# First transposes between products of ones, and the parts of x~ pinned in order

## Chip, cores and metric

The kernel runs on one core of a Trainium2 chip, as one launch. The metric is device microseconds of that core. PE is the matrix engine (PEld its weight loads), DVE, ACT and POOL are the vector, scalar and general engines, SP issues most of the DMAs.

## The reference

Two layers of a bidirectional encoder over x of 256 tokens by 1024 channels, all float32. Each layer has three stages, each with its own RMSNorm:

```
x += 0.5 * SwiGLU(RMSNorm(x))            # stage 3l:   1024 -> 2 x 2816 -> 1024
z  = RMSNorm(x) @ W_in                   # stage 3l+1: the mixer
x += concat(attention, pooling, HGRN2 of z) @ W_out
x += 0.5 * SwiGLU(RMSNorm(x))            # stage 3l+2
...
rmsnorm(x, g) = x * rsqrt(mean(x * x) + EPS) * g
swiglu(h)     = (silu(h @ w_gate) * (h @ w_up)) @ w_down
```

The change touches how x, times the gain g, gets to the matrix engine at the start of every stage, and the beginning of the program above all.

## The kernel before

**Products in three parts.** A float32 product is made as three products of a rounded format: each operand is split into a high part (ACT writes it, rounded) and a low part (DVE subtracts the high part from the original). Weights come from HBM in halves of 128 x 1024 (`feed_dma`, L133, SP queue, four `stage` buffers) and are split into `whi` (ACT, L149) and `wlo` (DVE, L150), up to `LOOK` = 4 halves ahead (`ahead`, `split_part`). The first half of all is fetched and split in two pieces. `mm3t` (L168 to L170) then makes high x high, high x low and low x high.

**x~, the turned activations.** At each stage x has to lie with its channels on the partitions. `turn(stage, dh, tt)` transposes four 128 x 128 tiles of one token half `tt` on PE (L294) into PSUM tiles `xps`; each `xps` tile is one bank and holds two channel tiles k of 256 tokens each: `xps[0]` has k = 0 and 1, `xps[1]` has 2 and 3. With the second token half, `turn` calls `parts` for its four k: ACT writes the high part `xh` = rounded x * g (L272), DVE the low part `xl` (L273); both read the bank. The normalising factor is left out of x~ and applied to the products later: `squares` (ACT, L281) sums x * x, `rms` makes `rc` of it, and the gate's Silu scales with `rc`. The fourth `squares` of a stage is followed by a preload of another activation table.

**PSUM.** A pool of four banks (`g`) serves `idle`, the `xps`, the accumulators `gu` (two a block, one for each token half), `hp` and others; a bank is given again when the readers of its last tile are done. At a later stage's start four `xps` tiles hold all four, and the next stage's first accumulators (`gu`, in the mixer `ga` and `gb`) take the first banks that come free.

**Order.** The instructions of PE and SP stand in the order in which they are written. Those of ACT and DVE are ordered by a planner when the program is built, from data dependences and its own costs; `issue_after(ins)` ties the instructions in its block that are on the engine of `ins` behind `ins`, without a semaphore.

**SwiGLU.** `ffn` runs over 11 blocks of 256 columns. `gate_up` makes one block's `gu` in four quarters of 12 products (two k, two token halves, three parts). Quarter q uses k = 2q and 2q + 1 and weight half i0 + q. In quarter 1 the held back `turn` of the second channel half runs (`late_turn`); in the first stage `sums`, which calls the four `squares`, is called in quarter 3. In the mixer, `proj_pair` starts with `ga` and `gb` side by side.

**The beginning** (`body`): twelve 128 x 128 products of ones into `idle` (two PE records each), the split of the first weight half, the two turns of the first channel half, DMAs up to half 5, then the first stage, with the second channel half in `second`.

Of the kernel before, what the change touches and what calls it, by code (L numbers as in the profile page):

```python
# [8 lines left out]
F32 = mybir.dt.float32  # L9
F32R = mybir.dt.float32r  # L10
U8 = mybir.dt.uint8
AF = mybir.ActivationFunctionType
ALU = mybir.AluOpType
# [3 lines left out]
P = 128  # L17
# [24 lines left out]
HALF = 1024  # L42
# [28 lines left out]
class Trunk:  # L71
    def __init__(self, ctx, tc, x_in, wall, prm_in, rel_in, cst_in, cst2_in, msk_in, band_in, y_out):
        self.tc, self.nc = tc, tc.nc
        self.wall, self.y_out = wall, y_out
        nc = self.nc
        pool = lambda name, bufs=1, **k: ctx.enter_context(tc.tile_pool(name=name, bufs=bufs, **k))
        self.cp = pool("const")
        self.stg = pool("stage", 4)
        self.whl = pool("whl", LOOK + 1)
        self.xp = pool("xp")  # L80
        self.wk = pool("wk", 2)
        self.mx = pool("mx")
        self.pg = pool("pg", 4, space=PSUM)
        self.py = pool("py", 4, space=PSUM)
        self.dr = pool("dr", space=DRAM)

        self.stage_t, self.split_t = {}, {}
        self.n_dma = 0
        self.n_split = 0
        self.cur = 0  # L90
        self.pending = self.then = None
        self.look = LOOK

        self.x = self.cp.tile([P, 2, D], F32, name="x")
        self.prm = self.cp.tile([P, N_PRM], F32, name="prm")
        self.cst = self.cp.tile([P, N_CST], F32, name="cst")
        self.msk = self.cp.tile([P, 2 * len(LEVELS), 64], U8, name="msk")
        self.ones = self.cp.tile([P, P], F32, name="ones")
        self.bias = self.cp.tile([P, 2, 8, T], F32, name="bias")
        self.lbc = self.cp.tile([P, 3, 4], F32, name="lbc")  # L100
        self.band = self.cp.tile([P, 4, 2, T], F32, name="band")
        self.qgs = self.cp.tile([P, 8], F32, name="qgs")

        xr = x_in.rearrange("p (t d) -> p t d", t=2)
        self.ident = self.cst[:, K_ID:K_ID + P]
        nc.scalar.dma_start(self.ident, cst_in[:, K_ID:K_ID + P])
        nc.scalar.dma_start(self.prm[:, 0:C_PW], prm_in[:, 0:C_PW])
        w0 = self.stage_t[0] = self.stg.tile([P, HALF], F32, tag="stage", name="stage")
        self.n_dma = 1
        for dh in range(2):  # L110
            s = slice(dh * 512, dh * 512 + 512)
            for tt in range(2):
                nc.sync.dma_start(self.x[:, tt, s], xr[:, tt, s])
            if dh == 0:
                for j in range(2):
                    q = slice(j * HALF // 2, (j + 1) * HALF // 2)
                    nc.sync.dma_start(w0[:, q], wall[0][:, q])
        self.feed_dma(2)
        self.prm_in, self.cst_in = prm_in, cst_in
        self.bones = self.cp.tile([P, P], F32R, name="bones")  # L120
        cols = self.cp.tile([P, 4], F32, name="cols")
        self.eps, self.one = (cols[:, n:n + 1] for n in range(2))
        nc.vector.memset(self.eps, EPS)
        nc.vector.memset(self.one, 1.0)
        nc.vector.memset(self.ones, 1.0)
        self.rel_in, self.cst2_in, self.msk_in, self.band_in = rel_in, cst2_in, msk_in, band_in
# [135 lines left out]
    def new_xt(self):  # L262
# [2 lines left out]
        self.ss = self.wk.tile([P, 64], F32, tag="ss", name="ss", bufs=2)[:, 0:4]  # L265
        self.xps = {}

    def parts(self, stage, k, src):

        nc = self.nc  # L270
        g = self.prm[:, C_GAIN + stage * 8 + k:C_GAIN + stage * 8 + k + 1]
        nc.scalar.activation(self.xh[:, k, :], src, AF.Copy, scale=g)  # L272
        nc.vector.scalar_tensor_tensor(self.xl[:, k, :], src, g, self.xh[:, k, :].bitcast(F32),  # L273
                                       op0=ALU.mult, op1=ALU.subtract)

    def squares(self, stage, dh, tt):

# [533 lines left out]
    def body(self):  # L811
        nc = self.nc
        self.new_xt()

        idle = self.pg.tile([P, 512], F32, tag="g", name="idle")
        for _ in range(12):
            self.nc.tensor.matmul(idle[:, 0:P], lhsT=self.ones, rhs=self.ones, start=True, stop=True)
        for j in range(2):
            self.split_part(0, j * HALF // 2, (j + 1) * HALF // 2)
        self.n_split = 1  # L820
        for tt in range(2):
            self.turn(0, 0, tt)
        self.feed_dma(5)

        def second():
            for tt in range(2):
                self.turn(0, 1, tt)

        def sums():
            for dh in range(2):  # L830
                for tt in range(2):
                    self.squares(0, dh, tt)

        self.pending, self.then, self.look = second, sums, 0
        for l in range(DEPTH):
            self.ffn(3 * l, self.to_stage(3 * l + 1))
            self.mixer(l)
            self.ffn(3 * l + 2, self.to_stage(3 * l + 3) if l + 1 < DEPTH else self.out_part)
# [131 lines left out]
```

## Time and profile before

| | |
|---|---|
| time, median of 3 runs | 1021.98 us (1021.69 to 1022.37) |
| profiled execution, its own time | 1022.51 us |
| its span, first to last instruction | 1020.7 us |
| busy PE / PEld | 1002.3 us (98%) / 828.2 us (81%) |
| busy DVE / ACT | 606.7 us (59%) / 538.7 us (53%) |
| DMA | 181.16 MB, mean 177 GB/s |

The busy time of an engine is the sum over its instructions, overlaps counted once; matrix products are pipelined and their ends are modelled. The engines' clocks aren't in it: the page gives the granted clock of PE by slices of the span, as 9 in tenths (90% or more) in all forty. Times of rows are counted from the span's start.

### The profile page before, as it was taken

The numbers are of one execution on the slowest core, as the hardware profiler recorded it, in microseconds if no ns is written. First come the engines' busy times: TensorE is split into PE (matmuls) and PEld (weight loads), VectorE is DVE, ScalarE is ACT, GpSimd is POOL, SyncE is SP. The second block draws the span as 40 slices with busy tenths as digits, with TensorE's granted clock in tenths as the row PEclk, the third lists the DMA queues.
The fourth block names the chain that finished last, engine by engine and source line by source line (L and its number), as shares of the span: only waits on it lengthen the run. The fifth ranks groups of instructions, "written<-read, shape, count | busy, mean of one in ns | idle before, by whom it ended". The sixth has DMA issues, their size and how long they took to land.

```text
span 1020.7 us, 14464 instructions
## 1 busy us (share of the span) xinstructions
PE 1002.3 (98%) x5722; PEld 828.2 (81%) x5722; DVE 606.7 (59%) x811; ACT 538.7 (53%) x774; POOL 3.3 (0%) x8
## 2 busy tenths in 40 slices
PE   8999999999999999999999999999999999999998
PEld 7888788897877888888878888888877778888886
DVE  5555555689955655555565454556998465545453
ACT  7444444675765544444474444446857554444441
POOL 0000100000000000000000000000000000000000
PEclk9999999999999999999999999999999999999999
DMA  7675876544334556555655656554542345556551
GB/s 257 223 258 187 278 257 187 181 148 151 103 107 155 173 186 194 185 194 185 186 165 186 186 188 185 192 188 135 192 142 88 121 155 190 186 188 187 186 187 60
DMA packets 50276, 181.16 MB, mean 177 GB/s; under 512 B 5752, under 2 KB 6008, under 8 KB 49952
## 3 DMA queue, kind: packets, MB, share of 16 engines
q1 hardware_dynamic: 48528, 174.09, 53.4%
q0 software_dynamic: 720, 4.21, 1.2%
q10 hardware_dynamic: 960, 1.94, 0.5%
q8 instruction: 45, 0.74, 0.3%
q14 instruction: 23, 0.19, 0.1%
HBM read 179.15 MB, written 3.16 MB: 179 GB/s over the span
## 4 chain that ended last, share of the span: by engine, by line
PE 84%; DVE 8%; ACT 4%; issue 2%; DMA 1%; SPq 0%; DVEq 0%
PE gu L168 16%; PE gu L170 15%; PE gu L169 15%; PE ya L170 8%; PE ya L168 8%; PE ya L169 8%; DVE wlo L150 2%; ACT whi L149 2%; PE hp L352 2%; PE wo L168 1%; PE wo L170 1%; PE wo L169 1%; DVE P L701 1%; PE xps L294 1%; PE pv L727 1%
## 5 line engine op out<-in xcount | busy, mean ns | idle before, releaser
L150 DVE TENSOR_TENSOR wlo<-stage,whi 128x1024 fp32r<-128x1024 f32 (+1 forms) x329 | 401.4, 1222 | 350.1 <-ACT whi L149 349.3
L149 ACT ACTIVATE whi<-stage 128x1024 fp32r<-128x1024 f32 (+1 forms) x329 | 347.1, 1056 | 369.2 <-PE gu L170 200.1
L168 PE MATMUL gu<-whi,xh 128*128 128x512 f32 x704 | 275.4, 391 | 3.7 <-DVE xl L273 2.2
L170 PE MATMUL gu<-whi,xl 128*128 128x512 f32 x704 | 274.2, 390 | 0.0
L169 PE MATMUL gu<-wlo,xh 128*128 128x512 f32 x704 | 274.0, 389 | 0.0
L168 PEld LDWEIGHTS gu<-whi,xh 128*128 128x128 f32 x704 | 132.2, 188 | 33.1 <-DVE xl L273 2.9
L170 PEld LDWEIGHTS gu<-whi,xl 128*128 128x128 f32 x704 | 132.1, 188 | 28.3 <-DVE xl L273 0.9
L169 PEld LDWEIGHTS gu<-wlo,xh 128*128 128x128 f32 x704 | 132.2, 188 | 27.0
L168 PE MATMUL ya<-whi,hi 128*128 128x512 f32 x352 | 141.5, 402 | 0.0
L170 PE MATMUL ya<-whi,lo 128*128 128x512 f32 x352 | 137.7, 391 | 0.0
L169 PE MATMUL ya<-wlo,hi 128*128 128x512 f32 x352 | 137.3, 390 | 0.0
L170 PEld LDWEIGHTS ya<-whi,lo 128*128 128x128 f32 x352 | 66.0, 188 | 14.4
L169 PEld LDWEIGHTS ya<-wlo,hi 128*128 128x128 f32 x352 | 66.3, 188 | 12.6
L168 PEld LDWEIGHTS ya<-whi,hi 128*128 128x128 f32 x352 | 66.2, 188 | 12.3
L345 ACT ACTIVATE g<-gu,rc 128x256 f32<-128x256 f32 x88 | 41.4, 475 | 47.4 <-PE gu L170 47.4
L346 DVE SCALAR_TENSOR_TENSOR h<-gu,rc,g 128x256 f32<-128x256 f32 x88 | 42.0, 481 | 23.9 <-ACT g L345 23.9
L258 DVE TENSOR_TENSOR lo<-hp,hi 128x512 fp32r<-128x512 f32 x44 | 30.1, 684 | 2.8 <-ACT hi L257 2.8
L257 ACT ACTIVATE hi<-hp 128x512 fp32r<-128x512 f32 x44 | 25.5, 580 | 2.7 <-PE hp L352 2.7
L352 PEld LDWEIGHTS hp<-cst,h 128*128 128x128 f32 x176 | 21.8, 139 | 5.7
L352 PE MATMUL hp<-cst,h 128*128 128x128 f32 x176 | 26.3, 271 | 0.0
L272 ACT ACTIVATE xh<-xps,prm 128x256 fp32r<-128x256 f32 x48 | 20.5, 471 | 5.8 <-DVE xl L273 3.4
L273 DVE SCALAR_TENSOR_TENSOR xl<-xps,prm,xh 128x256 fp32r<-128x256 f32 x48 | 21.3, 478 | 2.4 <-ACT xh L272 2.2
(223 smaller groups left out, 997.5 us busy)
## 6 DMA issues: line engine op xcount, KB each, us to landing
stage<-w_all SPq DMA_DIRECT2D x327, 512.0 KB, 3.5
skew<-drow POOLq DMA_DIRECT2D x1, 2048.0 KB, 10.3
bias<-skew POOLq DMA_DIRECT2D x2, 1024.0 KB, 11.6
x<-x SPq DMA_DIRECT2D x4, 256.0 KB, 5.1
band<-band ACTq DMA_DIRECT2D x1, 1024.0 KB, 7.7
y_t<-x SPq DMA_DIRECT2D x4, 256.0 KB, 2.2
stage<-w_all SPq DMA_DIRECT2D x2, 256.0 KB, 5.5
mskf<-msk ACTq DMA_DIRECT2D x1, 320.0 KB, 5.7
```

The costliest lines, as they stand in the source:

```text
L149: nc.scalar.activation(hi[:, s], st[:, s], AF.Copy)
L150: nc.vector.tensor_tensor(lo[:, s], st[:, s], hi[:, s].bitcast(F32), op=ALU.subtract)
L168: nc.tensor.matmul(out, lhsT=ah, rhs=wh, start=start, stop=False, skip_group_check=True)
L169: nc.tensor.matmul(out, lhsT=ah, rhs=wl, start=False, stop=False, skip_group_check=True)
L170: nc.tensor.matmul(out, lhsT=al, rhs=wh, start=False, stop=stop, skip_group_check=True)
L257: self.nc.scalar.activation(hi, src, AF.Copy)
L258: self.nc.vector.tensor_tensor(lo, src, hi.bitcast(F32), op=ALU.subtract)
L272: nc.scalar.activation(self.xh[:, k, :], src, AF.Copy, scale=g)
L273: nc.vector.scalar_tensor_tensor(self.xl[:, k, :], src, g, self.xh[:, k, :].bitcast(F32), op0=ALU.mult, op1=ALU.subtract)
L345: silu = nc.scalar.activation(g2[:, tt, :], gu[tt][:, 0:256], AF.Silu, scale=r)
L346: nc.vector.scalar_tensor_tensor(h[:, tt, :], gu[tt][:, 256:512], r, g2[:, tt, :], op0=ALU.mult, op1=ALU.mult)
L352: nc.tensor.transpose(hp[:, f, tt * P:tt * P + P], h[:, tt, f * P:f * P + P], self.ident)
```

## The change

The twelve products of ones become eight before the two first turns and four behind them. The split of the first weight half moves behind the turns in the program, and its `whi` are tied behind the last `xh`, its `wlo` behind the last `xl` (`behind`). `parts` ties every `xh` behind the `xh` before it and every `xl` behind the `xl` before it; `pins` is kept over all six stages. The first stage's four `squares` are tied behind the last `xh` of that stage. `held` is not used.

```diff
--- before.py
+++ after.py
@@ -89,6 +89,8 @@
         self.n_split = 0
         self.cur = 0
         self.pending = self.then = None
+        self.pins = [None, None]
+        self.held = None
         self.look = LOOK
 
         self.x = self.cp.tile([P, 2, D], F32, name="x")
@@ -265,13 +267,20 @@
         self.ss = self.wk.tile([P, 64], F32, tag="ss", name="ss", bufs=2)[:, 0:4]
         self.xps = {}
 
+    def behind(self, n):
+
+        return self.tc.issue_after(self.pins[n].ins) if self.pins[n] is not None else nullcontext()
+
     def parts(self, stage, k, src):
 
         nc = self.nc
         g = self.prm[:, C_GAIN + stage * 8 + k:C_GAIN + stage * 8 + k + 1]
-        nc.scalar.activation(self.xh[:, k, :], src, AF.Copy, scale=g)
-        nc.vector.scalar_tensor_tensor(self.xl[:, k, :], src, g, self.xh[:, k, :].bitcast(F32),
-                                       op0=ALU.mult, op1=ALU.subtract)
+        with self.behind(0):
+            hi = nc.scalar.activation(self.xh[:, k, :], src, AF.Copy, scale=g)
+        with self.behind(1):
+            lo = nc.vector.scalar_tensor_tensor(self.xl[:, k, :], src, g, self.xh[:, k, :].bitcast(F32),
+                                                op0=ALU.mult, op1=ALU.subtract)
+        self.pins = [hi, lo]
 
     def squares(self, stage, dh, tt):
 
@@ -813,13 +822,18 @@
         self.new_xt()
 
         idle = self.pg.tile([P, 512], F32, tag="g", name="idle")
-        for _ in range(12):
-            self.nc.tensor.matmul(idle[:, 0:P], lhsT=self.ones, rhs=self.ones, start=True, stop=True)
-        for j in range(2):
-            self.split_part(0, j * HALF // 2, (j + 1) * HALF // 2)
-        self.n_split = 1
+        def warm(n):
+            for _ in range(n):
+                nc.tensor.matmul(idle[:, 0:P], lhsT=self.ones, rhs=self.ones, start=True, stop=True)
+
+        warm(8)
         for tt in range(2):
             self.turn(0, 0, tt)
+        warm(4)
+        with self.behind(0), self.behind(1):
+            for j in range(2):
+                self.split_part(0, j * HALF // 2, (j + 1) * HALF // 2)
+        self.n_split = 1
         self.feed_dma(5)
 
         def second():
@@ -827,9 +841,10 @@
                 self.turn(0, 1, tt)
 
         def sums():
-            for dh in range(2):
-                for tt in range(2):
-                    self.squares(0, dh, tt)
+            with self.behind(0):
+                for dh in range(2):
+                    for tt in range(2):
+                        self.squares(0, dh, tt)
 
         self.pending, self.then, self.look = second, sums, 0
         for l in range(DEPTH):
```

## Rows read from the trace of the kernel before

**Rows 1.** the waits of PE by releaser: us in total, times, longest.

```profile
PE gu L168 <- DVE xl L273: 2.2, 3, 0.7
PE ga L161 <- DVE xl L273: 1.5, 2, 0.7
```

**Rows 2.** timeline of ACT and DVE, attention's query parts: start, us, instruction.

```profile
242.02 0.48 DVE L676 SCALAR_TENSOR_TENSOR Lq<-tp,qgs,Hq 128x256 fp32r<-128x256 f32 x1
...
242.54 0.47 ACT L675 ACTIVATE Hq<-tp,qgs 128x256 fp32r<-128x256 f32 x1 [2.21 <-DVE Lq L676]
...
243.05 0.48 DVE L676 SCALAR_TENSOR_TENSOR Lq<-tp,qgs,Hq 128x256 fp32r<-128x256 f32 x1
```

**Rows 3.** timeline of the beginning; behind the bracket, idle time and its releaser.

```profile
0.74 0.85 SPq L113 DMA_DIRECT2D x<-x  x2
...
1.12 5.49 PE L817 MATMUL idle<-ones 128*128 128x128 f32 x24 [1.12 <-DVE ones L125]
...
4.09 0.63 ACT L281 ACTIVATE sq<-x 128x512 f32<-128x512 f32 x1 [1.15 <-DMA x<-x]
...
7.07 1.30 ACT L149 ACTIVATE whi<-stage 128x512 fp32r<-128x512 f32 x2 [2.25 <-DMA stage<-w_all]
7.73 1.36 DVE L150 TENSOR_TENSOR wlo<-stage,whi 128x512 fp32r<-128x512 f32 x2 [1.48 <-ACT whi L149]
8.27 0.82 ACT L272 ACTIVATE xh<-xps,prm 128x256 fp32r<-128x256 f32 x2
...
8.78 0.50 PE L168 MATMUL gu<-whi,xh 128*128 128x512 f32 x1 [1.13 <-ACT xh L272]
...
12.36 1.03 PE L294 MATMUL xps<-cst,x 128*128 128x128 f32 x8
...
17.06 0.19 PEld L168 LDWEIGHTS gu<-whi,xh 128*128 128x128 f32 x1 [0.66 <-ACT xh L272]
...
17.27 3.17 ACT L149 ACTIVATE whi<-stage 128x1024 fp32r<-128x1024 f32 x3
```

**Rows 4.** the tile x, DMA issued between 1.1 and 1.5 us.

```profile
DMA to landing us min/median/max: 3.3/3.8/4.4
```

**Rows 5.** products of ones and turns: duration in ns, min/median/max.

```profile
L817 PE MATMUL idle<-ones x24: 421/421/580, 1.1 to 6.2; 128*128 128x128 f32 x24
...
L294 PE MATMUL xps<-cst,x x16: 270/272/421, 6.4 to 13.1; 128*128 128x128 f32 x16
```

**Rows 6.** timeline, start of the layer's second SwiGLU stage.

```profile
324.71 0.84 ACT L272 ACTIVATE xh<-xps,prm 128x256 fp32r<-128x256 f32 x2 [0.27 <-PE xps L294]
...
326.06 0.84 ACT L272 ACTIVATE xh<-xps,prm 128x256 fp32r<-128x256 f32 x2
...
326.33 0.69 DVE L371 SCALAR_TENSOR_TENSOR x<-wo,x 128x512 f32<-128x512 f32 x1 [0.23 <-PE wo L170]
...
326.94 0.86 DVE L273 SCALAR_TENSOR_TENSOR xl<-xps,prm,xh 128x256 fp32r<-128x256 f32 x2
327.46 0.50 PE L168 MATMUL gu<-whi,xh 128*128 128x512 f32 x1 [0.74 <-DVE xl L273]
...
327.87 1.23 DVE L150 TENSOR_TENSOR wlo<-stage,whi 128x1024 fp32r<-128x1024 f32 x1
...
328.95 0.39 PE L168 MATMUL gu<-whi,xh 128*128 128x512 f32 x1
```

**Rows 7.** timeline, start of the first mixer stage.

```profile
199.41 0.87 DVE L273 SCALAR_TENSOR_TENSOR xl<-xps,prm,xh 128x256 fp32r<-128x256 f32 x2
199.95 0.39 PE L161 MATMUL ga<-xh,whi 128*128 128x256 f32 x1 [0.74 <-DVE xl L273]
...
200.77 0.28 PE L161 MATMUL gb<-xh,whi 128*128 128x256 f32 x1
```

**Rows 8.** timeline, later in the same SwiGLU stage's first block.

```profile
333.70 1.06 ACT L149 ACTIVATE whi<-stage 128x1024 fp32r<-128x1024 f32 x1
...
334.67 0.45 ACT L272 ACTIVATE xh<-xps,prm 128x256 fp32r<-128x256 f32 x1
```

## The prediction

> **What bounds the kernel now.** I read the page first: PE is busy 1002.3 of 1020.7 us, so a change to the inputs of the first products, or to those of each stage's first products, is worth what it moves on PE. The list of PE's waits then says where PE stands idle: at the five later stage starts, three of them SwiGLU stages and two mixers, the first product waits 0.7 us each time for an x~ low part on DVE [rows 1]. The timelines show why. PE's order is fixed. The parts of four tiles k0 to k3 fill two PSUM banks, xps0 with k0 and k1, xps1 with k2 and k3. The third pair of parts, not the second, is the one that PE waits for at a SwiGLU start (third xl from 326.94, about 0.48 long, first product 327.46) [rows 6]. This is k1: only k0 and k1 together free the bank that `gu[0]` takes. So the planner runs k0, k2, k1, k3, alternating banks. The reason stands in the attention's query parts, the same two instructions with two halves in one bank: low part at 242.02 for 0.48, then the second high part at 242.54, marked as released by that low part after 2.21 us of idling, then its low part at 243.05 [rows 2]. The program does not let ACT read a bank while DVE still reads it: in one bank high, low, high, low go strictly in turn, 0.51 us a step.
>
> **The change, part by part.** *The pins.* `parts` now chains its high parts in the order k0, k1, k2, k3, and its low parts too, in all six stages, not in the first alone. Worked from the step of 0.51 and the lengths 0.47 and 0.48 of one [rows 2], and the spacings 0.37 and 0.38 of neighbouring xh and xl in different banks (0.84 and 0.86 for two) [rows 6]: xh0 at 0, xl0 0.51, xh1 1.02, xl1 1.53, xh2 1.39, xl2 1.91 to 2.39, xh3 2.43, xl3 2.94 to 3.42. In the alternating order all four low parts can be done at 2.4. The pinned order takes about 1.0 us longer for four tiles, and ACT's queue holds still behind each waiting high part.
>
> *The start.* The ones: 24 records last 5.49 us [rows 3], about 0.22 apart, so eight products, 16 records, leave PE at 4.6 instead of 6.2. The turns' second piece of x is asked for second of the pair at 0.74 to 1.59, near 1.2 [rows 3], and takes 4.4 [rows 4], so it lands near 5.5; four turns run before it and four after, and bank xps0 is full near 6.2 (5.55, 0.22 to the second of these turns, and its own 0.42 [rows 5]). xh0 starts at 6.25 instead of 8.27. So far this is 2 us early. The four products of ones behind the turns take 8 x 0.22 = 1.8 us, from 6.4 to 8.2, and nothing on PE is ready by then; they cost nothing. But the weights' parts are now behind the whole chain: xh3 ends at 6.25 + 2.43 + 0.47 = 9.15, xl3 at 9.67. Two whi halves (1.30) and two wlo halves (1.36) [rows 3] then end near 10.3 and 11.1. The first product goes at 9.8, after the first whi half (0.65), 1.0 later than 8.78. The first tile's second product with wlo waits for 11.1, and eight products at 0.23 end the quarter near 13.0, where the second turns now begin at 12.36 [rows 3]: +0.65. Against it, the weight load at 17.06 that idled 0.66 for xh [rows 3] has its input: the second turn's chain starts near 13.9, its second tile is done 2.0 later at 15.9, and the third quarter wants it past 17. That gives back 0.5. Net +0.15; below, -0.1 (the 0.66 whole, and a tenth in the halves' overlap), above, the clock case among the rivals.
>
> *Squares last.* Four squares of 0.63, one of which now runs at 4.09 in ACT's idle time [rows 3], go behind xh7: 2.6 us of ACT from about 17. There ACT now runs three weight conversions, 3.17 us from 17.27 [rows 3]. If all four squares go first, the fifth half's whi (1.06) ends near 21 and its wlo (1.23 [rows 6]) near 22.7, where PE wants it soon after 17.06 + 21 x 0.23 = 21.9: 0 to 0.8. Nothing in the trace of before decides whether the planner lets the conversion in between, so I take the middle, +0.4. The statistics behind the squares still have a block of 8 us of PE work before their lateness would reach PE.
>
> *The later stage starts.* At the SwiGLU start at 324.71 the third low part is held by the residual add at 326.33 as now [rows 6], so `gu[0]` still starts near 327.46. `gu[1]`, due six products later at 328.95, needs xps1, hence xl3. That now ends at 327.8. In the pinned order xl2 ends there, xh3 follows at 327.85 and xl3 from 328.36 to 328.84: just in time, 0. But if ACT puts its waiting square, and DVE its waiting wlo of 1.23 from 327.87, before them, xl3 ends near 329.4: +0.5. In the mixer the second accumulator `gb` is wanted only 0.82 after `ga` (200.77 after 199.95), and xl3 ends now at 199.41 + 0.87 = 200.28 [rows 7]. With the chain alone xl3 ends near 201.3 and `gb` starts 0.6 late; with a wlo ahead of it near 201.9, 1.2 late. For the planner's habit I have one place: a fourth high part ran at 334.67, after a conversion begun at 333.70 [rows 8]; it fills a wait with what is ready, and that speaks for the upper ends. Since its times are not the chip's, I take the middle of each: 3 x 0.27 = 0.8 and 2 x 0.9 = 1.8. PE has no slack to take these back; each is a shift of all that follows. The second halves, k4 to k7, I cost at nothing: twelve products of 0.23, 2.7 us, lie between their turn and their first use, and two tiles of a chain take 2.0; without that cover a step of 0.5 per stage is the price.
>
> **The sum.** 0.15 + 0.4 + 0.8 + 1.8 = +3.15 us. The profiled execution took 1022.51 (span 1020.70 and 1.81 around it), so it would become 1025.7; the median of the three runs is 0.53 lower, and on that footing I forecast 1025.1, slower by 0.3%. Less than 0.2%, some 2 us, can't be told from no change.
>
> [...]
>
> **Rivals.**
> 1. *The chain runs undisturbed, and the time falls.* If at each SwiGLU start DVE takes xl1 ahead of the add, xps0 is free at 326.7, `gu[0]` starts at 326.8, and an unbroken chain ends at 324.71 + 3.42 = 328.13, before `gu[1]` wants its bank at 328.3. That gains 0.65 three times, 0.05 at two mixers, and with the squares slipping in, the start is even: 1022.0 - 2.1 = 1019.9. It decides once xl3 ends before 328.3. For it: program order puts the parts ahead of the add; against it: the add ran first, at 326.33, with the third high part begun at 326.06 [rows 6]. Chance 0.10.
> 2. *The chain alone, nothing slips between.* SwiGLU starts 0, mixers 2 x 0.6, start 0.15, squares 0.4: +1.75, with squares hidden +1.35: about 1023.5, within 0.2%. For it: that conversions slip in rests on one place [rows 8]. Chance 0.28.
> 3. [...] Chance 0.17.
> 4. *The forecast*, conversions between the pinned parts at some of the five starts: 0.42; its own range is 1024.1 to 1026.9. The rest, 0.03, is other reorderings by the planner, of either sign.
>
> **The numbers.** Faster by over 0.2% is rival 1, 0.10. Rival 2 makes 0.28 for no change. The forecast, the late clock and the rest make 0.62 for slower. The range runs from 1021.3, between rivals 1 and 2 where a tenth is left out, to 1028.4, the late clock with all upper ends (0.15 + 0.8 + 1.5 + 2.4 + 2.0 = 6.85 above the median less half a microsecond of overlap), where another tenth is.
>
> **What would show it.** Right: in the start, xh1 released by xl0, the four xh some 2.9 us from first start to last end, the first product near 9.8; at the mixers `gb` over 1.4 us after `ga`; at SwiGLU starts the seventh product later than 1.5 us after the first, waiting for xl. Wrong: xh1 next to xh0 without a wait (no bank rule), `gu[0]` at once after the third turns, or the second turns in the start before 12.36. [...] The forecast falls if the mixers' `gb` is not late, since they carry more than half of it.

## The result and the profile after

The changed kernel takes 1031.49 us (median of four runs, 1030.02 to 1031.66) against 1022.17 (1021.69 to 1022.48) for the kernel before on the same chip: ratio 1.0089, 95% interval 1.0076 to 1.0102. It is slower by 9.3 us; forecast were 3.1, and the range ended at 1028.4. The profiled execution took 1031.66 with a span of 1029.9, so its span is 9.2 us longer than the one of before.

The page looks almost as before (PE busy 1005.1 us instead of 1002.3). To find where the time went, I set the two traces side by side product by product: both make the same products of PE in the same order, so the start of a product after, less its start before, is how late PE is by then. The columns are the start in the trace of before, the row is the lateness in us:

```
product of before at   8.78  17.06  27.59  199.95  210.02  321.05  345.05  505.14  530.11  690.19  720.08  822.02  845.16
after                  2.07   2.83   3.14    3.13    5.91    5.86    6.50    6.52    7.12    7.14    8.41    8.61    9.16
```

So 3.1 us go in the first 28, 2.8 at the first mixer's start (199.95 to 210.02), 0.6 at each of three SwiGLU starts (321 to 345, 505 to 530, 822 to 845), 1.3 at the second mixer's start (690 to 720), and 0.2 in the second layer's attention (between 720 and 822). Elsewhere nothing is lost, and nothing is taken back. The 0.2 also stands in the profiled executions of `e1`, `e3`, `e6` and `e7` below and in none of the others: the attention's first scores wait 0.60 for a low part of the keys on DVE there (0.45 before). Why that part is later stays open.

**The start.** The waits of PE (engine, what it waited for, and us in total, times, longest) name the places, to be held against [rows 1]:

```profile
PE gu L170 <- ACT whi L151: 3.5, 1, 3.5
PE gu L170 <- DVE xl L281: 2.2, 3, 0.7
...
PE gb L163 <- DVE rc L312: 2.1, 2, 1.0
...
PE ga L163 <- DVE xl L281: 1.5, 2, 0.7
...
PE gu L170 <- DVE rc L312: 1.0, 3, 0.4
```

The two rows of [rows 1] are still there, at 0.7 each. The other three are new: one long wait for the first weights, and waits of the second accumulators `gb` and `gu`, put down to `rc`. That `rc` is the first small step of the normalising factor on DVE (`rms`), 0.15 long, which stands right behind the fourth low part in DVE's queue. The accumulator doesn't read `rc`; its bank is free when the fourth low part is done. The timeline of the beginning (start, us, instruction; in brackets the idle time before it and its releaser) stands against [rows 3]:

```profile
5.84 0.65 PE L303 MATMUL xps<-cst,x 128*128 128x128 f32 x4 [0.74 <-DMA x<-x]
6.06 1.28 ACT L279 ACT_TABLE_LOAD   x1 [6.06 <-DMA prm<-params]
6.33 1.06 PE L827 MATMUL idle<-ones 128*128 128x128 f32 x8
...
7.36 0.47 ACT L279 ACTIVATE xh<-xps,prm 128x256 fp32r<-128x256 f32 x1
...
8.38 0.84 ACT L279 ACTIVATE xh<-xps,prm 128x256 fp32r<-128x256 f32 x2 [0.55 <-DVE xl L281]
...
9.80 0.47 ACT L279 ACTIVATE xh<-xps,prm 128x256 fp32r<-128x256 f32 x1 [0.58 <-DVE xl L281]
...
10.85 0.57 PE L170 MATMUL gu<-whi,xh 128*128 128x512 f32 x1 [3.46 <-ACT whi L151]
...
12.16 0.63 PE L172 MATMUL gu<-whi,xl 128*128 128x512 f32 x1
...
12.59 0.63 PE L170 MATMUL gu<-whi,xh 128*128 128x512 f32 x1
...
15.58 1.04 PE L303 MATMUL xps<-cst,x 128*128 128x128 f32 x8
```

The turns are done near 6.5, as forecast. But ACT's first instruction is now `xh` itself, and the load of ACT's function table (1.28) goes ahead of the first activation and behind its wait for the gains (6.06). Before, a square was first, and its table was loaded while ACT waited for x:

```profile
1.66 1.28 ACT L281 ACT_TABLE_LOAD   x1 [1.66 <-PEq L962]
```

So xh0 starts at 7.36, not 6.25. The chain goes as worked out: the second high part waits 0.55 for the first low part, the fourth 0.58 for the third, and xh0 to the end of xh3 takes 2.91 (forecast 2.9). Then the products go 0.43 apart instead of 0.23. The windows (PE, PEld, DVE, ACT and POOL busy, with instructions; the granted clock of PE; DMA) show the clock that goes with it:

```profile
core 0: us, PE busy (x) PEld busy (x) DVE busy (x) ACT busy (x) POOL busy (x), PEclk, DMA share, GB/s
7.20:10.60 3.40, 0.19 (x2) 0.00 (x0) 1.65 (x4) 2.26 (x6) 0.00 (x0) 1.00 1.04 420
10.60:14.20 3.60, 3.20 (x7) 2.33 (x8) 3.40 (x5) 3.55 (x5) 0.00 (x0) 0.57 0.52 149
14.20:18.00 3.80, 3.80 (x21) 3.17 (x21) 2.88 (x4) 1.46 (x3) 0.00 (x0) 0.96 0.89 304
```

The four products of ones behind the turns took 1.06 us and not 1.8, and then PE stood still for 3.46 us. The mean granted clock of the next stretch is 0.57: its products start 0.42 to 0.43 apart from 12.16 to 14.30, and 0.23 apart again from 14.65 on. The second turns start at 15.58 instead of 12.36, 3.22 late: 2.07 until the first product and 1.15 in the slow first quarter. Then 0.4 comes back where before idled for `xh`, and 0.3 goes when a low part of the second chain is late.

**The later starts.** The first mixer's start, to be held against [rows 7]:

```profile
202.55 0.87 DVE L281 SCALAR_TENSOR_TENSOR xl<-xps,prm,xh 128x256 fp32r<-128x256 f32 x2
203.08 0.38 PE L163 MATMUL ga<-xh,whi 128*128 128x256 f32 x1 [0.74 <-DVE xl L281]
203.12 0.63 ACT L290 ACTIVATE sq<-x 128x512 f32<-128x512 f32 x1
203.34 1.22 DVE L152 TENSOR_TENSOR wlo<-stage,whi 128x1024 fp32r<-128x1024 f32 x1
203.74 0.47 ACT L279 ACTIVATE xh<-xps,prm 128x256 fp32r<-128x256 f32 x1
204.47 0.48 DVE L281 SCALAR_TENSOR_TENSOR xl<-xps,prm,xh 128x256 fp32r<-128x256 f32 x1
204.86 0.15 DVE L312 TENSOR_TENSOR rc<-ss 128x2 f32<-128x2 f32 x1
...
205.09 0.36 PE L163 MATMUL gb<-xh,whi 128*128 128x256 f32 x1 [1.03 <-DVE rc L312]
```

The window behind it, in the columns of the windows above:

```profile
205.00:209.00 4.00, 3.91 (x20) 3.94 (x21) 1.84 (x14) 1.08 (x5) 0.00 (x0) 0.58 0.37 131
```

While the fourth high part waits for the third low part, ACT takes a square (203.12) and DVE a weight's low part of 1.22 (203.34). The fourth low part then starts at 204.47, and `gb` goes 2.01 after `ga` instead of 0.82: 1.2 lost. Behind that wait the clock fell too (0.58), which took 2.8 - 1.2 = 1.6 more: the lateness jumps from 3.13 to 4.33 at `gb`'s first product, stays near 4.40 for four more, and then grows by 0.09 with nearly every product to 5.92. A SwiGLU start, against [rows 6], has the same three instructions between the parts:

```profile
333.33 0.51 PE L170 MATMUL gu<-whi,xh 128*128 128x512 f32 x1 [0.74 <-DVE xl L281]
333.37 0.63 ACT L290 ACTIVATE sq<-x 128x512 f32<-128x512 f32 x1
333.58 1.21 DVE L152 TENSOR_TENSOR wlo<-stage,whi 128x1024 fp32r<-128x1024 f32 x1
333.98 0.47 ACT L279 ACTIVATE xh<-xps,prm 128x256 fp32r<-128x256 f32 x1
334.71 0.48 DVE L281 SCALAR_TENSOR_TENSOR xl<-xps,prm,xh 128x256 fp32r<-128x256 f32 x1
...
335.34 0.47 PE L170 MATMUL gu<-whi,xh 128*128 128x512 f32 x1 [0.34 <-DVE rc L312]
```

`gu[1]` starts 2.01 after `gu[0]` instead of 1.49 (from 327.46 to 328.95), 0.52 late.

### The profile page after: what moved, and what is told of

Its sections match the earlier page's. It is cut to its first block, busy times and chain, and to the rows that moved or that the text cites. A ratio compares the mean times of both kernels' runs of the same rounds, so it can differ in the third digit from the quotient of the medians.

```text
span 1029.9 us, 14462 instructions
## 1 busy us (share of the span) xinstructions
PE 1005.1 (98%) x5722; PEld 829.5 (81%) x5722; DVE 606.4 (59%) x811; ACT 538.9 (52%) x774; POOL 3.3 (0%) x8
## 4 chain that ended last, share of the span: by engine, by line
PE 83%; DVE 10%; ACT 4%; issue 2%; DMA 1%; ACTq 0%; DVEq 0%
PE gu L170 15%; PE gu L172 15%; PE gu L171 15%; PE ya L172 8%; PE ya L170 8%; PE ya L171 8%; DVE wlo L152 3%; ACT whi L151 2%; PE hp L361 2%; PE wo L170 1%; PE wo L172 1%; PE wo L171 1%; DVE xl L281 1%; PE xps L303 1%; DVE P L710 1%
```

## The experiments

Theory: the pinned order makes two engines meet in one bank at every step, and what slips between the steps delays the second accumulator at five starts; in the start a table load and PE's clock come on top. Rivals: the pins themselves cost nothing, and the ones or the squares do it; or the clock alone. Each experiment is held against the kernel before, run beside it.

**Pins in the first stage alone.** `e1` is the changed kernel with `parts` pinned only in stage 0:

```diff
-        with self.behind(0):
+        first = stage == 0
+        with self.behind(0) if first else nullcontext():
...
-        with self.behind(1):
+        with self.behind(1) if first else nullcontext():
```

> The parts are pinned in the first stage alone; the later five stages are free again, the beginning is that of the changed kernel. Bank theory (pinned k order makes ACT and DVE take turns in one PSUM bank): the later shifts go (0.5 us at each of three SwiGLU starts, 1.2 to 1.3 at each of two mixers, the 1.6 of a slower clock behind the first mixer), gb again 0.8 us after ga, and only the beginning's 3.1 us stay: about 1025.3 us. Rival (the loss is made in the beginning and only carried on, or by a planner disturbed everywhere): the time stays within 1 us of 1031.5.

Measured: 1025.4 us (1025.36 to 1026.36) against 1022.18; 1.0034 [1.0021, 1.0047]. PE is 2.82 late at 27.59 and 2.95 at 845.16. All later starts are as before; the mixer's `gb` follows `ga` by 0.82 again:

```profile
202.76 0.38 PE L163 MATMUL ga<-xh,whi 128*128 128x256 f32 x1 [0.74 <-DVE xl L282]
...
203.58 0.28 PE L163 MATMUL gb<-xh,whi 128*128 128x256 f32 x1
```

**Pins in the later stages alone.** `e2` is the kernel before, with the pins of `parts` only for `stage > 0`; its start is untouched.

```diff
+        later = stage > 0
+        with self.behind(0) if later else nullcontext():
...
+        with self.behind(1) if later else nullcontext():
```

> The beginning is that of the kernel before (twelve ones, free squares and parts), the five later stages are pinned. Bank theory: SwiGLU starts +0.5 each, mixers +1.2 to 1.3 each, 4.0 us together, and up to 1.6 more where the clock falls behind the first mixer: 1026.2 to 1027.8. Rival (beginning only): 1022.2.

Measured: 1027.51 (1026.33 to 1028.19); 1.0049 [1.0032, 1.0066]. Start -0.2, mixer +2.8, +0.6, +0.6, mixer +1.3, +0.6. The costs of `e1` and `e2` nearly add up to the change's: by the medians 3.2 + 5.3 = 8.5 of 9.3 us, in the profiled executions 2.95 + 5.66 = 8.6 of 9.2. (The profiled one of `e2` was the longest of its four.) The pins of the later stages are the larger part, and they need nothing of the new start.

**Is it the bank, or the order?** `e3` is the changed kernel with every pin kept, but with k0 and k2 in one bank and k1 and k3 in the other:

```diff
-            if tt == 0 and j % 2 == 0:
-                self.xps[k // 2] = self.pg.tile([P, 2, T], F32, tag="g", name="xps")
-            nc.tensor.transpose(self.xps[k // 2][:, j % 2, ...
+            if tt == 0 and j < 2:
+                self.xps[2 * dh + j] = self.pg.tile([P, 2, T], F32, tag="g", name="xps")
+            nc.tensor.transpose(self.xps[2 * dh + j % 2][:, j // 2, ...
...
-                self.parts(stage, k, self.xps[k // 2][:, k % 2, :])
+                self.parts(stage, k, self.xps[2 * dh + k % 2][:, k % 4 // 2, :])
```

> The changed kernel, but neighbouring tiles lie in different PSUM banks (k0 and k2 in one, k1 and k3 in the other), so that the same pinned order k0, k1, k2, k3 changes banks at each step. Bank theory: no high part waits for the low part before it, four tiles take about 2.4 us and not 3.4, later stages cost nothing against before (first product within 0.1 us of its old lateness, gb 0.8 us behind ga), the beginning 1 us less or more if the clock holds: 1023 to 1024.5. Rival (a pinned order costs as such, whatever the bank): as the changed kernel, 1030 to 1031.7.

Measured: 1023.95 (1022.51 to 1024.42); 1.0016 [1.0007, 1.0026]. The later starts cost nothing any more: PE is 1.77 late at 27.59 and 1.92 at 845.16. The same pinned order of the same parts costs 0.5 to 2.8 at a later start in one layout and nothing in the other, so it is the shared bank. What is left is lost in the start, where PE pauses for 2.42 and the clock falls as in the changed kernel (granted 0.60 from 10.6 to 14.2, there 0.57). The parts now run side by side:

```profile
8.33 0.87 ACT L279 ACTIVATE xh<-xps,prm 128x256 fp32r<-128x256 f32 x2 [0.19 <-DVE xl L281]
```

A high part waits 0.55 to 0.58 in the start of the changed kernel, where two neighbours share a bank, and 0.19 here, where they don't.

**The ones alone.** `e4` is the kernel before with eight products of ones ahead of the turns and four behind:

```diff
+        warm(8)
...
         for tt in range(2):
             self.turn(0, 0, tt)
+        warm(4)
```

> The kernel before with eight ones ahead of the first turns and four behind them; ACT and DVE keep the order of the kernel before. Bank theory: the first product waits for the same xh and weights, the pause between ones and first product is under 2 us: 1022.0, within 0.5 us. Rival (turns between ones let the clock fall or rise late): products 0.43 us apart for a few us after the first, 1023.5 or more.

Measured: 1021.85 (1021.65 to 1022.65); 0.9999 [0.9990, 1.0009]: no change, and PE 0.7 early in the profiled execution. Turns and ones here (duration in ns, min/median/max, first and last start):

```profile
L818 PE MATMUL idle<-ones x24: 274/421/582, 1.1 to 7.4; 128*128 128x128 f32 x24
...
L294 PE MATMUL xps<-cst,x x8: 421/421/421, 4.7 to 6.2; 128*128 128x128 f32 x8
```

All eight turns take 421 ns here, and the ones behind them come down to 274. Turns between the ones left the time where it was.

**The table load.** `e5` adds one small activation to the changed kernel, so that the table is loaded ahead of the wait for the gains:

```diff
+        nc.scalar.activation(cols[:, 2:3], self.one, AF.Copy)
```

> The changed kernel with one more ACT instruction at the very beginning, a copy of one column of ones, so that the activation table is loaded while ACT is idle and not behind the wait for the gains. [...] Rival (something else, such as the landing of the first weights, sets the first product): unchanged, 1031.5.

Measured: 1031.53 (1029.58 to 1032.75); 1.0092 [1.0077, 1.0108]: no gain on the changed kernel. The profiled execution, 1029.58, was the shortest of the four. The table load came early, at 1.66, and xh0 at 6.25, but the time did not follow:

```profile
1.66 1.28 ACT L128 ACT_TABLE_LOAD   x1 [1.66 <-PEq L978]
...
6.25 0.47 ACT L280 ACTIVATE xh<-xps,prm 128x256 fp32r<-128x256 f32 x1 [3.10 <-PE xps L304]
```

And two of its waits of PE:

```profile
PE gu L171 <- ACT whi L152: 2.2, 1, 2.2
...
PE hp L362 <- DVE h L356: 0.8, 1, 0.8
```

The first product comes 1.1 earlier, after 2.2 us of pause, and the clock falls all the same (granted 0.50 from 10.0 to 13.4). And PE now waits 0.84 for `h` near 30 us, which the changed kernel does not: something else is late by nearly as much as the start was.

**Ones without a gap.** `e6` is the changed kernel with `warm(14)` in place of `warm(4)`, so PE has ones until its weights come.

> [...] If the pause of 3.5 us is what lets the clock fall, the products behind it stand 0.23 us apart and not 0.43, the first quarter ends 1.1 us earlier: 1030.3. Rival (the clock falls for what turns and ones are, or in any case there): still 0.43 apart, 1031.5.

Measured: 1030.91 (1030.14 to 1032.83); 1.0094 [1.0078, 1.0111], no clear gain on the changed kernel. The clock holds, and PE is 1.20 late at 17.06 instead of 2.83:

```profile
7.20:10.60 3.40, 2.82 (x27) 2.63 (x25) 1.87 (x5) 2.27 (x6) 0.00 (x0) 1.00 1.00 392
10.60:14.20 3.60, 3.38 (x15) 2.55 (x16) 3.43 (x4) 3.31 (x4) 0.00 (x0) 1.00 0.53 176
```

So with the pause filled (0.58 of it left, against 3.46) the granted clock stayed at 1.00, where the changed kernel has 0.57. Of the 1.63 gained, 0.25 was there at the first product, because the gains came 0.25 sooner and the table load with them (5.81 instead of 6.06); the clock cost the other 1.4. Yet by 27.59 PE is 2.97 late again: it waits for a late low part of the second channel half (0.7 lost near 20.5 of the columns above), then 0.8 for `h`.

**Table and ones together.** `e10` has the edits of `e5` and `e6`.

> The changed kernel with the activation table loaded early and fourteen products of ones behind the turns. Theory: the first product comes near 9.7, the clock holds, products stand 0.23 us apart, and PE is only about 0.5 us behind the kernel before when its third quarter ends; but the squares behind xh7, the table load behind them and the statistics still give the first block's Silu its time, and the turn of the first block's h near 30 us waits for it as before, so that PE is 2.5 to 3 us behind from there and the time stays near that of the table or the ones alone: 1029.5 to 1031. Rival (the beginning's loss was table and clock alone): 2.5 us off the changed kernel, 1028.8 with the clock held behind the first mixer and down to 1027.3.

Measured: 1030.37 (1029.8 to 1031.31) against 1022.34; 1.0080 [1.0063, 1.0096]. PE is 0.49 late at 17.06 and 2.83 at 27.59. One wait of PE, for a low part of the second channel half (0.2 in the changed kernel), and the chain behind another, that for `h`:

```profile
PE gu L173 <- DVE xl L282: 0.6, 1, 0.6
```

```profile
23.04 1.28 ACT L295 ACT_TABLE_LOAD   x1
...
24.34 1.06 ACT L152 ACTIVATE whi<-stage 128x1024 fp32r<-128x1024 f32 x1
...
27.69 1.28 ACT L355 ACT_TABLE_LOAD   x1
28.99 0.84 ACT L355 ACTIVATE g<-gu,rc 128x256 f32<-128x256 f32 x2
...
29.49 0.88 DVE L356 SCALAR_TENSOR_TENSOR h<-gu,rc,g 128x256 f32<-128x256 f32 x2 [0.56 <-ACT g L355]
...
30.13 0.85 PE L362 MATMUL hp<-cst,h 128*128 128x128 f32 x4 [0.84 <-DVE h L356]
```

Squares behind the eighth high part (20.12, itself late), then two table loads with three weight conversions between them (24.34, 25.49 and 26.61), `rc`, the Silu at 28.99, `h`, and `hp` cannot turn `h` before 30.13; before, `hp` ran without a wait:

```profile
27.49 0.60 PE L352 MATMUL hp<-cst,h 128*128 128x128 f32 x4
```

So under these pins the late squares set a floor of about 2.7 us under the first stage, which in the changed kernel the table load and the lost clock cover. On the way to it PE loses 0.9 around that late low part. In `e3`, with the same tie of the squares, they begin at 18.07 instead of 21.48, and PE, 1.8 late, doesn't wait for `h`: that speaks for the shared banks behind the floor too.

**Squares freed, and squares sooner.** `e7` is the changed kernel without the `with self.behind(0)` around the squares. `e11` is `e10` with the squares tied behind a piece of the first weight half, where `held` is the second `whi` of it:

```diff
+        held = self.held
...
-            with self.behind(0):
+            with self.tc.issue_after(held.ins):
```

> The changed kernel without the tie of the first stage's squares; the order on ACT then begins with the table load and a square, as in the kernel before, and the squares fill the waits of the pinned parts. If squares last costs by the late table load and by ACT work moved behind xh7, the first product comes near 9.8 and the time falls by 1 to 2 us: 1029.5 to 1030.5. Rival (the squares are off the path): 1031.5, within half a microsecond.

> The kernel with early table and fourteen ones, and the first stage's squares tied behind the first weight half's whi instead of behind xh7. If the squares behind xh7 are what holds the turn of the first block's h, it no longer waits, PE is 0.3 to 1 us behind there, and 1.5 to 2.5 us come off against the kernel with early table and ones alone. Rival (something else holds it): the same lateness near 30 us, the same time.

`e7`: 1032.18 (1031.63 to 1032.94); 1.0101 [1.0086, 1.0116]. This missed. The squares slip between the pinned high parts, xh3 starts at 9.30, the first product comes at 10.33 after a pause of 3.11, and from the sixth on the products go 0.41 to 0.43 apart: 3.05 late at 27.59. (Its profiled execution also lost 2.8, not 1.3, at the second mixer.) `e11`: 1029.19 (1027.44 to 1029.31); 1.0061 [1.0046, 1.0076]. PE is 0.53 late at 27.59, and `hp` has no wait:

```profile
28.02 0.60 PE L362 MATMUL hp<-cst,h 128*128 128x128 f32 x4
```

The late low part is gone with the sooner squares too. That confirms the floor: with table, clock and squares mended, the start costs 0.5, and what is left of the 4.9 is at the later starts. The profiled execution of `e11`, 1027.44, was the shortest of its four; where the others, 1029.11 to 1029.31, lost 1.7 more isn't known. Sooner squares alone, or with only one of the other two cures, were not tried.

**A version that beats both.** `e8` is the kernel before with the layout of `e3` alone. `e9` adds to it, at each later start, that ACT's square of the piece (1, 0) (second channel half, first token half) and DVE's residual add of the last piece (1, 1) are tied behind the parts, the square behind the last `xh`, the add behind the last `xl` (`pins` holds them; nothing else is pinned):

```diff
+        with self.tc.issue_after(self.pins[1].ins) if (dh, tt) == (1, 1) and post != self.out_part else nullcontext():
             self.nc.vector.scalar_tensor_tensor(s, y, by, s, op0=ALU.mult, op1=ALU.add)
...
+            if (dh, tt) == (1, 0):
+                with self.tc.issue_after(self.pins[0].ins):
+                    self.squares(stage, dh, tt)
```

> The kernel before, nothing pinned, with neighbouring tiles in different PSUM banks (k0 and k2 in one, k1 and k3 in the other). Bank theory: the planner still alternates banks, which now means k0, k1, k2, k3; the later stages stay as they are, and in the beginning the second tile's parts come one place earlier: the waits at 10.1 (0.4) and at 17.06 (0.4 to 0.6) shrink: 1021.2 to 1022.0. Rival (the planner's order is not about banks): some other order of parts, a shift at the later stages of either sign.

> The kernel with alternating banks, and at each later stage's start the third square is tied behind the last xh of the first four tiles and the fourth residual add behind their last xl, so that the chain of parts runs undisturbed. Theory: the first bank is free 0.6 to 0.7 us sooner at each of five starts: 3 us off, 1018 to 1019. Rival (the add is on the path itself, the turns of the last quarter wait for it): no gain, 1021 to 1023.

`e8`: 1021.58 (1020.95 to 1021.68) against 1021.81; 0.9997 [0.9988, 1.0006], no measurable change. `e9`: 1018.39 (1018.19 to 1018.95); 0.9967 [0.9954, 0.9979], 3.4 us faster than the kernel before. It gains 0.55 to 0.6 at each of the five later starts, 2.8 in all, as the wait of 0.7 in [rows 1] became 0.17:

```profile
323.81 0.86 ACT L272 ACTIVATE xh<-xps,prm 128x256 fp32r<-128x256 f32 x2 [0.19 <-DVE xl L273]
...
324.32 0.87 DVE L273 SCALAR_TENSOR_TENSOR xl<-xps,prm,xh 128x256 fp32r<-128x256 f32 x2 [0.15 <-ACT xh L272]
324.85 0.50 PE L168 MATMUL gu<-whi,xh 128*128 128x512 f32 x1 [0.17 <-DVE xl L273]
...
325.11 0.68 DVE L373 SCALAR_TENSOR_TENSOR x<-wo,x 128x512 f32<-128x512 f32 x1
```

The residual add that held the third low part in [rows 6] now runs behind it. The lateness of the other kernels, in the same columns as above (negative is early):

```
product of before at   8.78  17.06  27.59  199.95  210.02  321.05  345.05  505.14  530.11  690.19  720.08  822.02  845.16
e1 first stage pins    1.97   2.49   2.82    2.82    2.81    2.78    2.80    2.80    2.79    2.79    2.80    2.97    2.95
e2 later stage pins   -0.23  -0.23  -0.23   -0.23    2.54    2.51    3.14    3.16    3.78    3.80    5.08    5.08    5.66
e3 banks alternate     0.99   1.99   1.77    1.79    1.79    1.75    1.78    1.77    1.76    1.76    1.78    1.95    1.92
e4 ones only          -0.68  -0.69  -0.70   -0.70   -0.72   -0.75   -0.74   -0.75   -0.72   -0.72   -0.73   -0.69   -0.72
e5 table early         0.97   1.70   2.66    2.71    3.97    3.93    4.57    4.59    5.20    5.22    6.48    6.48    7.06
e6 ones long           1.82   1.20   2.97    3.02    4.28    4.28    4.91    4.93    5.54    5.56    6.82    7.01    7.60
e7 squares free        1.55   2.51   3.05    3.05    4.30    4.26    4.88    4.91    5.52    5.54    8.31    8.52    9.11
e8 before, banks      -0.34  -0.79  -1.01   -1.00   -1.01   -1.08   -1.04   -1.04   -1.06   -1.06   -1.05   -1.01   -1.01
e9 parts first        -0.90  -1.18  -1.40   -1.97   -1.98   -2.04   -2.60   -2.60   -3.19   -3.19   -3.75   -3.75   -4.31
e10 table and ones     1.12   0.49   2.83    2.90    4.15    4.12    4.74    4.76    5.37    5.39    6.65    6.66    7.25
e11 squares sooner     0.88   0.56   0.53    0.53    1.80    1.79    2.42    2.44    3.05    3.07    4.33    4.33    4.91
```

A mixer start costs 1.25 to 1.27 in `e5`, `e6`, `e10` and `e11` and about 2.8 where the granted clock read 0.58 and 0.57 behind `gb` (after and `e2`, both at the first): the same wait, with or without the clock. In `e7`, which lost 2.8 at the second, the clock was not read there. These rows are one execution each, so the 1.5 us of such a fall are luck of the profiled run, and the medians decide on totals.

## Why the prediction was right in direction and too small

The sum was 3.15 and the profiled execution lost 9.16. Of the 6.0 between them the start made 2.6, the two mixers 2.3, the three SwiGLU starts 1.0, and 0.2 came in the second attention, where nothing was forecast.

**The bank and the pins: right.** xh1 was released by xl0 after a wait of 0.55, the four high parts took 2.91 (2.9 forecast), the alternating layout of `e3` took the cost away.

**The three SwiGLU starts: mechanism right, size off.** The term was 0.27 each, for the middle of 0 and 0.5 (which is 0.25). Measured 0.64, 0.60 and 0.55, 1.8 in all against 0.8. A square and a `wlo` did slip into the wait at every one of them, so the upper end, and a little more, was the value; with the planner's one shown habit pointing there [rows 8], the middle had no ground.

**The two mixers: mechanism right, size off, and a step missing.** 0.9 each was forecast, 1.2 the upper end. `gb` came 1.2 late, again the upper end. Not foreseen was that the clock falls behind the pause before `gb` in some executions (granted 0.58 in after, 0.57 in `e2`), 1.5 to 1.6 more: after lost 2.8 and 1.3 against 1.8 in sum.

**The start: failed.** Forecast +0.15 and +0.4, measured 3.1. Three steps failed. First, "xh0 starts at 6.25": the table load was taken for gone with the square it stood before, but it moved behind the gains' wait (+1.1). Second, "1.8 us, from 6.4 to 8.2": the ones took 1.06 and left PE idle for 3.46, and behind that pause the granted clock read 0.57 and the products stood over 0.4 apart. Ahead of it the turns took 272 ns at their median. The quarter took 4.7 instead of the 3.2 forecast, 1.5 more; against `e6` the clock is 1.4 of it. Third, "a block of 8 us of PE work before their lateness would reach PE": the chain of squares, two table loads, weight conversions, `rc`, Silu and `h` is longer than that cover, and with table and clock mended PE waits for it at 30.13 (`e10`); `e11` removed it. In the changed kernel itself PE was late enough not to wait. Looked for was a late weight conversion, +0.4, and that was not what bound. These three overlap: mending the first, or the second, or both leaves 2.7 to 3.0 at 27.59, and all three bring it to 0.5. With them mended the first sum comes out: in `e11` the first product is at 9.66 and the second turns at 13.02, where 9.8 and 13.0 were forecast; only 0.1 of the 0.5 to be given back at 17.06 came. The second halves, costed at nothing, lost 0.3 at one late low part in the start of the changed kernel and 0.7 and 0.9 in `e6` and `e10`, where PE gets there sooner: weight conversions slip between those parts, so two tiles took longer than the 2.0 that were set against the cover. At the later stages they cost nothing visible.

**The rivals.** The undisturbed chain did not happen at any of the five starts. The chain alone did not either. The 2.0 us that the upper end of the range holds for a late clock is shown by no run; what the runs showed in its place is the granted clock of 0.57 behind the pause, which cost 1.4 in the start (after against `e6`). What decided, slower, got 0.62.

## What to carry to other kernels

Before an order is pinned, look at which neighbours in it share a PSUM bank: the pins of the later stages cost 5.3 us by the medians where consecutive parts met in one bank (`e2`), and nothing where the tiles alternated (`e3`). When the first activation of a program changes, ask what its function table load now stands behind (1.28 us, at 6.06 in after and at 1.66 in `e5`), and fill PE's pause with products until the real ones come (granted clock 1.00 in `e6`, 0.57 in after), then look for the next chain in line: here three delays lay over one another, and neither the table, nor the ones, nor both together brought back more than 1.3 of the 9.3 us. Where a waiting engine may take something else, price the term at the longest thing that is ready, not at the middle.

## What the hardware showed that was not expected

PE's granted clock read low behind some pauses and not behind others. Behind pauses of 3.46, 2.42 and 2.18 us before the first product (after, `e3`, `e5`) it read 0.57, 0.60 and 0.50, and the products stood 0.42 to 0.43 apart; behind 3.11 in `e7` they stood 0.41 to 0.43 apart, and behind about 2.9 in `e1` (an estimate: ones until 7.9, the first product at 10.75) the clock read 0.57. Behind 1.13 (before), 0.58 (`e6`) and 0.44 (`e4`) they stood 0.22 to 0.24 apart, with a granted clock of 1.00 in `e6` and `e4`, and in `e8` the fourth and fifth stood 0.23 apart behind a pause of 2.09:

```profile
8.44 0.50 PE L168 MATMUL gu<-whi,xh 128*128 128x512 f32 x1 [2.09 <-ACT xh L272]
```

In `e3` and `e7` the third to fifth product behind the pause still stood 0.23 to 0.24 apart, and from the sixth on they went 0.41 to 0.43 apart. At the first mixer's `gb` a pause of 1.03 behind a first one of 0.74 was followed by a granted clock of 0.58 in the profiled execution of after and 0.57 in that of `e2`; at the same place `e5`, `e6`, `e7`, `e10` and `e11` lost only the wait. So it is shown that the clock held in the start once its pause was filled (1.00 in `e6`); why it falls behind the same pause in one execution and not in another is not. Within the pause itself the granted clock reads 1.00 (after, 7.2 to 10.6).

At the beginning the products of ones and the turns grow shorter, from 421 ns to some 272, at another time in each of these executions, with the ones started at 1.1 in all. In after all eight first turns, from 4.5 on, took 272 to 328 ns; in before [rows 5] the turns started 0.21 to 0.22 apart up to 6.82 and 0.11 to 0.12 apart behind that; in `e4` all eight took 421, and only ones behind them were shorter; in `e8`, which has the ones and turns in the order of before, the last five ones stood 0.11 apart from 4.75 on and every turn took 272 or 273. So tenths of a microsecond in the start, such as the 1.0 of `e8`'s span, are no finding.

The 1.28 us of the first table load were hidden or not, by what the first activation waited for: it was at 1.66 in `e5` and at 6.06 in after.
